# Gated units transposed four blocks at a time, query and key products ahead of value products in the last opening blocks, one activation-table load fewer, and retention's scale issued later

## The chip, the cores and the metric

One NeuronCore of a Trainium2 chip runs the whole program. The metric is the device time of one execution in microseconds (us). The profile calls the engines PE (TensorE), ACT (ScalarE), DVE (VectorE), POOL (GpSimd) and SP (SyncE, which issues the loads); PEld is TensorE's weight load.

## What is computed

A trunk of two layers over 256 tokens of width 1024, in float32. Each layer has a mixer and a gated feed-forward network, both behind an RMS norm and a modulation by a conditioning vector `c`:

```python
for layer in range(2):
    shift_m, scale_m, gate_m, shift_f, scale_f, gate_f = ada_mod(c, ada_w[layer], ada_b[layer])
    h = modulate(rms_norm(x, norm_gains[layer, 0]), shift_m, scale_m)
    y = attn_hybrid_mixer(h, ...) if layer == 0 else retention_mixer(h, ...)
    x = x + gate_m * y
    h = modulate(rms_norm(x, norm_gains[layer, 1]), shift_f, scale_f)
    gt, up = split(h @ w_gate_up[layer], 2)          # 2 x 2816 columns
    x = x + gate_f * ((silu(gt) * up) @ w_down[layer])
out = rms_norm(x, final_norm)
```

The attention mixer has 8 stick-breaking heads (queries, keys and values qs, ks, vs) and 8 rotary softmax heads (qm, km, vm). The retention mixer has 4 heads; each head's output o is normalised over its 512 columns, `(o - mu) * rsqrt(var + 1e-5)`, multiplied by a gain and by `silu(g)`, and goes into the output projection.

## The kernel before

**Tiles and products.** The tokens are two halves of 128, t = 0 and t = 1. A weight unit is 256 rows by 512 columns, two row blocks of 128 wide as one raw tile of 128x1024. To keep float32 precision on TensorE, every operand is split in two fp32r parts: ScalarE copies `wh` out of the raw tile (L221), VectorE takes `wl = raw - wh` (L222), each 512 columns at a time. A row block's product is three matmuls into one accumulator: wh with hh (L440), wl with hh (L441) and wh with hl (L444), where hh and hl are the two parts of the activations. These three lines are most of TensorE's time.

**Stages, with their times in the profiled execution.** Opening, 0 to 68 us: the row blocks kb = 0 to 7 of qs, ks and vs (g = 0, 1, 2), each block's products following as soon as its modulated activations and its split weights are there. Attention, to 161 us: the stick-breaking scores (`sb_task`: L590, L598, then Abs, Exp and Ln on ScalarE at L602 to L604, the maximum on VectorE at L605), the projections qm, km, vm, the softmax part (`moba_part`, transposes at L661) and the output projection. The first feed-forward network, to 355 us, with 11 groups of gated units and then the down projection. Retention, to 536 us: for each of 4 heads the projections rqk, rg, rv and a task for each half (`ret_task`), then the output projection to 560 us. The second feed-forward network, to 751 us.

**Small work between products.** A generator (a task) holds the work that follows a group: transposes, scores, splits. `yield 4` puts a task off by four ticks; each weight unit of each half makes two ticks, one after its first products and one after its L444s, and a task whose count has run out issues its next piece there. `GY`, `R0` to `R2`, `QP` and `SY` are such counts. TensorE's order is therefore the order in which the program is written and ticks. The orders of ScalarE, VectorE, GpSimd and SyncE are made by a list scheduler when the program is built; only what `pin` or `keep_in_program_order` encloses keeps its place.

**The places of the change.** `products(kb, g)` issues the products of block kb for one of qs, ks and vs, both halves. `to_T` (L506, L507) transposes finished queries and keys to the form that the scores want: four transposes, and a copy on ScalarE (L507); for qs and ks a copy out of the accumulator (L515) goes ahead of them. `log_table` issues a load of ScalarE's activation table (L235) with the set that has exp and ln. `gu_post` takes an accumulator of gated units (256 gate columns, 256 up columns): Silu on ScalarE (L802), multiply on VectorE (L803), and `GY` ticks later a run of two transposes (L813) and a split into the activations of the down projection. `ret_task` ends with the normalisation: VectorE takes the moments, GpSimd works out the reciprocal root in steps of one column (`rsqrt`, L207 to L216), ScalarE multiplies by it (L758), and `R2` ticks later TensorE transposes the result.

The weight and ada loads go out on SyncE's one queue: L424 for weight units, L335 for blocks of `ada_w`. VectorE multiplies those `ada_w` blocks by c (L357, 128x1024 each), in between the other work.

Of the kernel before, what the change touches and what calls it, by code (L numbers as in the profile page):

```python
# [14 lines left out]
AF = mybir.ActivationFunctionType  # L15
# [4 lines left out]
P = 128  # L20
# [3 lines left out]
KD = D // P  # L24
# [10 lines left out]
MY, MV = (8, 6), 2  # L35
SY, SV = (7, 7), 4
GY = 4
R0, R1, R2 = 6, 4, 14
QR, QP = 6, 3
GW = 12  # L40
PRIO = 600
# [11 lines left out]
def trunk_kernel(  # L53
# [6 lines left out]
    nc = tc.nc  # L60
# [172 lines left out]
    def log_table():  # L233
        tc.keep_in_program_order(
            nc.scalar.preload_act_table_set("natural_log_exp_and_others"))  # L235
# [331 lines left out]

    def sb_task(t):
        if t == 0:
            log_table()  # L570
        if t == 0:
            st[t]["o"] = tuple(hp.tile([P, KD, P], F32R, tag="oq" + n, name=nm("o" + n))
                               for n in "hl")
        else:
            o = ap.tile([P, 2, KD, P], F32R, tag="B1l", name="o1")
            st[t]["o"] = o[:, 0], o[:, 1]
# [142 lines left out]
    def ret_task(h, t):  # L719
# [35 lines left out]
        v1 = sp.tile([P, 1], F32, tag="v", name=nm("v"))  # L755
        nc.gpsimd.tensor_scalar(v1, mv[:, 1:2], 1e-5, None, op0=ALU.add)
        r = rsqrt(v1)
        nc.scalar.activation(o, o, AF.Copy, scale=r)  # L758
        yield R2
        yield ("ps", 1, 1)  # L760
# [32 lines left out]
        return Blocks(f"{t}h", n), Blocks(f"{t}l", n)  # L793

    def gu_post(l, g):
        key = f"act{l}"

        def f(t, ps):
            if g == 0:
                st[t][key] = act_tiles(t, 22)  # L800
            s = w2(t)
            nc.scalar.activation(s[:, :256], ps[:, :256], AF.Silu)  # L802
            nc.vector.tensor_mul(s[:, :256], s[:, :256], ps[:, 256:])  # L803
            release(1)
            spawn(task(t, s))

        def task(t, s):
            hi, lo = st[t][key]
            yield GY
            yield ("ps", 1, 1)  # L810
            p = pt()
            for j in range(2):
                nc.tensor.transpose(p[:, j * P:(j + 1) * P], s[:, j * P:(j + 1) * P], ident)  # L813
            split(hi[:, 2 * g:2 * g + 2, :].rearrange("p k q -> p (k q)"),
                  lo[:, 2 * g:2 * g + 2, :].rearrange("p k q -> p (k q)"), p[:, :256])
            release(1)
            flags.add((t, key, 2 * g))
            flags.add((t, key, 2 * g + 1))

        return f  # L820

# [253 lines left out]
    def more(upto):  # L1075
        while ready[0] < min(upto, n):
# [6 lines left out]
                ada_load(*e)  # L1083
            ready[0] += 1

    def products(kb, g, ts=(0, 1)):
        kp, j = divmod(kb, 2)
        for t in ts:
            units[g * NP + kp][1](t, *ws[kp, g], js=(j,))

    strict[0] = True
    log_table()
# [124 lines left out]
```

## Time and profile before

| | |
|---|---|
| time, median of 3 runs | 761.07 us (760.92 to 762.19) |
| profiled execution | 761.21 us |
| its span on the chip | 759.4 us |
| TensorE busy | 732.6 us, 96% of the span |
| VectorE busy | 559.7 us, 74% |
| ScalarE busy | 403.2 us, 53% |
| GpSimd busy | 56.4 us, 7% |

A row of the timeline or a group gives its engine, line, operation and the program's names with the buffer numbers left out; `[1.25 <-ACT w L515]` says that the engine stood idle for 1.25 us before the row and that the idle time ended with ScalarE's write of `w` at line 515. Matmuls overlap their neighbours: the distance between two starts is what one costs, not the duration printed. The profiled execution lasts 1.8 us longer than its span, and it is 0.14 us above the median of the runs.

### The profile page before, as it was taken

The numbers are of one execution on the slowest core, as the hardware profiler recorded it, in microseconds if no ns is written. First come the engines' busy times: TensorE is split into PE (matmuls) and PEld (weight loads), VectorE is DVE, ScalarE is ACT, GpSimd is POOL, SyncE is SP. The second block draws the span as 40 slices with busy tenths as digits, with TensorE's granted clock in tenths as the row PEclk, the third lists the DMA queues.
The fourth block names the chain that finished last, engine by engine and source line by source line (L and its number), as shares of the span: only waits on it lengthen the run. The fifth ranks groups of instructions, "written<-read, shape, count | busy, mean of one in ns | idle before, by whom it ended". The sixth has DMA issues, their size and how long they took to land.

```text
span 759.4 us, 10601 instructions
## 1 busy us (share of the span) xinstructions
PE 732.6 (96%) x3598; PEld 581.2 (77%) x3598; DVE 559.7 (74%) x963; ACT 403.2 (53%) x836; POOL 56.4 (7%) x137
## 2 busy tenths in 40 slices
PE   8998997999999999999999999999999999999995
PEld 4776775667888878877788877777877888888884
DVE  3668999689898879857857777676588767665553
ACT  5339745665555545546545454454575555555541
POOL 1001000120000010001011111203020000000000
PEclk9999999999999999999999999999999999999999
DMA  9997889568999979946564737577747777655501
GB/s 297 346 360 253 288 291 331 184 185 271 335 295 342 330 246 326 341 168 194 191 199 146 241 120 224 185 236 240 234 146 224 224 228 213 192 178 181 171 1 55
DMA packets 116998, 174.91 MB, mean 230 GB/s; under 512 B 7640, under 2 KB 73376, under 8 KB 116944
## 3 DMA queue, kind: packets, MB, share of 16 engines
q1 hardware_dynamic: 115568, 171.86, 69.6%
q10 hardware_dynamic: 816, 1.60, 0.6%
q0 software_dynamic: 560, 0.77, 0.3%
q8 instruction: 28, 0.46, 0.3%
q14 instruction: 26, 0.21, 0.1%
HBM read 173.16 MB, written 1.05 MB: 229 GB/s over the span
## 4 chain that ended last, share of the span: by engine, by line
PE 65%; DVE 6%; ACT 2%; issue 2%; POOL 2%; DMA 1%; DVEq 0%; SPq 0%; ACTq 0%; POOLq 0%
PE acc L440 20%; PE acc L444 20%; PE acc L441 20%; DVE wl L222 2%; PE pt L813 1%; ACT wh L221 1%; ACT w L287 1%; DMA raw<-in_ffn_w_gate_up_dram 1%; DVE w L528 0%; PE pt L729 0%; PE pt L746 0%; POOL ra L211 0%; PE pt L506 0%; DVE w L256 0%; ACT w L227 0%
## 5 line engine op out<-in xcount | busy, mean ns | idle before, releaser
L222 DVE TENSOR_TENSOR wl<-raw,wh 128x512 fp32r<-128x512 f32 x456 | 298.0, 688 | 133.6 <-ACT wh L221 131.3
L221 ACT ACTIVATE wh<-raw 128x512 fp32r<-128x512 f32 x456 | 266.2, 623 | 210.0 <-PE acc L444 110.1
L440 PE MATMUL acc<-wh,hh 128*128 128x512 f32 x640 | 258.1, 403 | 3.3 <-ACT hh L963 2.2
L441 PE MATMUL acc<-wl,hh 128*128 128x512 f32 x640 | 250.5, 391 | 0.2 <-DVE wl L222 0.2
L444 PE MATMUL acc<-wh,hl 128*128 128x512 f32 x640 | 204.9, 395 | 1.2 <-DVE hl L291 1.2
L440 PEld LDWEIGHTS acc<-wh,hh 128*128 128x128 f32 x640 | 120.5, 188 | 32.4 <-ACT hh L963 3.8
L444 PEld LDWEIGHTS acc<-wh,hl 128*128 128x128 f32 x640 | 119.1, 188 | 28.2 <-DVE hl L291 2.7
L441 PEld LDWEIGHTS acc<-wl,hh 128*128 128x128 f32 x640 | 120.7, 189 | 24.4 <-DVE wl L222 1.3
L440 PE MATMUL acc<-wh,act 128*128 128x512 f32 x240 | 94.4, 393 | 0.0
L441 PE MATMUL acc<-wl,act 128*128 128x512 f32 x240 | 93.7, 390 | 0.2 <-DVE wl L222 0.2
L444 PE MATMUL acc<-wh,act 128*128 128x512 f32 x240 | 74.2, 390 | 0.0
L357 DVE SCALAR_TENSOR_TENSOR aacc<-raw,sc,aacc 128x1024 f32<-128x1024 f32 x48 | 61.4, 1279 | 0.0
L440 PEld LDWEIGHTS acc<-wh,act 128*128 128x128 f32 x240 | 45.1, 188 | 10.3 <-issue 0.8
L441 PEld LDWEIGHTS acc<-wl,act 128*128 128x128 f32 x240 | 45.1, 188 | 10.0 <-DVE wl L222 0.8
L444 PEld LDWEIGHTS acc<-wh,act 128*128 128x128 f32 x240 | 44.9, 188 | 9.4
L357 DVE SCALAR_TENSOR_TENSOR gate<-raw,sc,gate 128x1024 f32<-128x1024 f32 x32 | 40.9, 1279 | 0.1
L802 ACT ACTIVATE w<-acc 128x256 f32<-128x256 f32 x44 | 16.9, 384 | 28.1 <-PE acc L444 28.1
L803 DVE TENSOR_TENSOR w<-w,acc 128x256 f32<-128x256 f32 x44 | 18.4, 417 | 10.3 <-ACT w L802 10.2
L354 POOL MEMSET aacc<- 128x1024 f32 x6 | 5.6, 966 | 226.8 <-PE pt L387 178.6
L227 ACT ACTIVATE w<-x 128x512 f32<-128x512 f32 x20 | 12.5, 625 | 16.4 <-DVE x L309 15.7
L230 POOL TENSOR_SCALAR ss<-ss 128x1 f32<-128x1 f32 x8 | 2.3, 288 | 250.3 <-ACT w L227 250.3
L758 ACT ACTIVATE w<-w,ry 128x512 f32<-128x512 f32 x8 | 5.8, 724 | 27.3 <-POOL ry L216 27.3
(168 smaller groups left out, 622.0 us busy)
## 6 DMA issues: line engine op xcount, KB each, us to landing
raw<-in_ffn_w_gate_up_dram SPq DMA_DIRECT2D x176, 256.0 KB, 4.3
raw<-in_ada_w_dram SPq DMA_DIRECT2D x80, 512.0 KB, 5.5
raw<-in_ffn_w_down_dram SPq DMA_DIRECT2D x44, 512.0 KB, 5.1
raw<-in_ret_w_in_dram SPq DMA_DIRECT2D x32, 512.0 KB, 3.8
early<-in_ada_w_dram SPq DMA_DIRECT2D x16, 512.0 KB, 7.4
raw<-in_ret_w_in_dram SPq DMA_DIRECT2D x32, 256.0 KB, 3.9
raw<-in_ret_w_o_dram SPq DMA_DIRECT2D x16, 512.0 KB, 5.1
raw<-in_att_w_qkv_dram SPq DMA_DIRECT2D x24, 256.0 KB, 7.2
```

What stands on the lines that cost most here:

```text
L221: pin(nc.scalar.activation(hi, src, AF.Copy))
L222: pin(nc.vector.tensor_tensor(lo, src, hi, op=ALU.subtract))
L227: pin(nc.scalar.activation(w2(t), xt[t][:, half * 512:(half + 1) * 512], AF.Square, scale=1.0 / 32.0, accum_out=ss))
L287: nc.scalar.activation(hs[1][:, c], ps[1][:, c], AF.Identity, scale=gm[:, 4 + j:5 + j], bias=sm[:, 4 + j:5 + j])
L357: tc.keep_in_program_order(nc.vector.scalar_tensor_tensor(a, r, sc[:, kk:kk + 1], a, op0=ALU.mult, op1=ALU.add))
L440: nc.tensor.matmul(ps, hi[:, kb, :], a, start=first, stop=False)
L441: nc.tensor.matmul(ps, hi[:, kb, :], b, start=False, stop=False)
L444: nc.tensor.matmul(ps, lo[:, kb, :], wh[:, j * 512:(j + 1) * 512], start=False, stop=last)
L758: nc.scalar.activation(o, o, AF.Copy, scale=r)
L802: nc.scalar.activation(s[:, :256], ps[:, :256], AF.Silu)
L803: nc.vector.tensor_mul(s[:, :256], s[:, :256], ps[:, 256:])
L813: nc.tensor.transpose(p[:, j * P:(j + 1) * P], s[:, j * P:(j + 1) * P], ident)
```

## The change

It has four parts. In the last two opening blocks (kb = 6 and 7) the value products are held back, and both blocks' are issued after block 7's queries and keys. The call of `log_table` in `sb_task` goes away; the one at the start of the program and those in `resid_post` stay. Two neighbouring gated units of a half share one 512-column tile, and one task transposes and splits all four of its blocks (the last unit, g = 10, is alone and keeps two). In `ret_task` a wait of 8 ticks stands ahead of the scale and `R2` is 6 ticks in place of 14.

```diff
-R0, R1, R2 = 6, 4, 14
+R0, R1, R2 = 6, 4, 6
...
     def sb_task(t):
-        if t == 0:
-            log_table()
...
         r = rsqrt(v1)
+        yield 8
         nc.scalar.activation(o, o, AF.Copy, scale=r)
         yield R2
...
     def gu_post(l, g):
+
         key = f"act{l}"
+        c = slice(g % 2 * 256, g % 2 * 256 + 256)
 
         def f(t, ps):
             if g == 0:
                 st[t][key] = act_tiles(t, 22)
-            s = w2(t)
-            nc.scalar.activation(s[:, :256], ps[:, :256], AF.Silu)
-            nc.vector.tensor_mul(s[:, :256], s[:, :256], ps[:, 256:])
+            if g % 2 == 0:
+                st[t]["gu"] = w2(t)
+            s = st[t]["gu"][:, c]
+            nc.scalar.activation(s, ps[:, :256], AF.Silu)
+            nc.vector.tensor_mul(s, s, ps[:, 256:])
             release(1)
-            spawn(task(t, s))
-
-        def task(t, s):
+            if g % 2 or g == 10:
+                spawn(task(t, st[t]["gu"], 2 * (g - g % 2), 2 + g % 2 * 2))
+
+        def task(t, s, b0, n):
             hi, lo = st[t][key]
             yield GY
             yield ("ps", 1, 1)
             p = pt()
-            for j in range(2):
+            for j in range(n):
                 nc.tensor.transpose(p[:, j * P:(j + 1) * P], s[:, j * P:(j + 1) * P], ident)
...
+    held = []
+
     def products(kb, g, ts=(0, 1)):
-        kp, j = divmod(kb, 2)
-        for t in ts:
-            units[g * NP + kp][1](t, *ws[kp, g], js=(j,))
+        if g == 2 and kb >= KD - 2:
+            held.append(kb)
+            if kb + 1 < KD:
+                return
+        for kb in held if g == 2 and held else (kb,):
+            kp, j = divmod(kb, 2)
+            for t in ts:
+                units[g * NP + kp][1](t, *ws[kp, g], js=(j,))
```

**TensorE at the end of the opening.** `acc_242` and `acc_288` are the query accumulators of the two halves, `acc_246` and `acc_313` those of the keys, `acc_250` and `acc_317` those of the values. Before, block 6's value products stand ahead of block 7's first query products (wh_627):

```order
L441 MATMUL acc_313<-wl_632,hh_239 128x512
L444 MATMUL acc_313<-wh_631,hl_240 128x512
L440 MATMUL acc_250<-wh_635,hh_166 128x512
L441 MATMUL acc_250<-wl_636,hh_166 128x512
L444 MATMUL acc_250<-wh_635,hl_167 128x512
L440 MATMUL acc_317<-wh_635,hh_239 128x512
L441 MATMUL acc_317<-wl_636,hh_239 128x512
L444 MATMUL acc_317<-wh_635,hl_240 128x512
L440 MATMUL acc_242<-wh_627,hh_166 128x512
L441 MATMUL acc_242<-wl_628,hh_166 128x512
L444 MATMUL acc_242<-wh_627,hl_167 128x512
L440 MATMUL acc_288<-wh_627,hh_239 128x512
```

In the changed kernel block 7's queries and keys come first, and then the two value accumulators take block 6 and block 7, one behind the other. The twelve rows ahead of and with the first score (L588, before L590); `pt_765` and `pt_774` are the transposes of the keys of the two halves:

```order
L506 MATMUL pt_765<-mats,w_0_145_742 128x128 x4
L444 MATMUL acc_250<-wh_635,hl_167 128x512
L440 MATMUL acc_317<-wh_635,hh_239 128x512
L441 MATMUL acc_317<-wl_636,hh_239 128x512
L506 MATMUL pt_774<-mats,w_1_147_753 128x128 x4
L444 MATMUL acc_317<-wh_635,hl_240 128x512
L440 MATMUL acc_250<-wh_635,hh_166 128x512
L441 MATMUL acc_250<-wl_636,hh_166 128x512
L444 MATMUL acc_250<-wh_635,hl_167 128x512
L440 MATMUL acc_317<-wh_635,hh_239 128x512
L441 MATMUL acc_317<-wl_636,hh_239 128x512
L588 MATMUL pt_789<-att_sb 128x128
```

The six matmuls of block 6's values have moved behind block 7's keys, and the second half's key transposes (`pt_774`), which stood directly ahead of the first score, now have six matmuls between them and it.

**ScalarE at retention's scale in a task of t = 1, first head.** `wh` are weight splits, and the row with `ry` is the scale by the reciprocal root. Before:

```order
L507 ACTIVATE qk_818_3984<-pt_832_4040 128x4x128
L221 ACTIVATE wh_850_4102<-raw_822_3999 128x512
L221 ACTIVATE wh_853_4122<-raw_833_4046 128x512
L758 ACTIVATE w2_1_840_4071<-w2_1_840_4071,ry_848_4089 128x512
L221 ACTIVATE wh_853_4122<-raw_833_4046 128x512
L221 ACTIVATE wh_859_4150<-raw_849_4100 128x512 x2
L706 ACTIVATE sg_855_4135<-acc_825_4007 128x512
```

After, the same stretch:

```order
L507 ACTIVATE qk_798_3943<-pt_812_3999 128x4x128
L221 ACTIVATE wh_830_4060<-raw_802_3958 128x512
L221 ACTIVATE wh_833_4080<-raw_813_4005 128x512 x2
L757 ACTIVATE w2_1_820_4030<-w2_1_820_4030,ry_828_4048 128x512
L221 ACTIVATE wh_839_4109<-raw_829_4058 128x512 x2
L704 ACTIVATE sg_835_4094<-acc_805_3966 128x512
```

One weight split of 128x512 (the second half of one weight tile, wh_853 before and wh_833 after) has come from behind the scale to ahead of it; all else in the stretch keeps its place.

**SyncE's queue at 90 us.** L424 loads attention weights, L335 loads blocks of `ada_w`. Before:

```order
L424 DMA raw_1018<-in_att_w_qkv_dram 128x2x512
L335 DMA raw_973<-in_ada_w_dram 128x1024
L424 DMA raw_1053<-in_att_w_qkv_dram 128x2x512
L335 DMA raw_1027<-in_ada_w_dram 128x1024
L335 DMA raw_1030<-in_ada_w_dram 128x1024
L424 DMA raw_1094<-in_att_w_qkv_dram 128x2x512
L335 DMA raw_1062<-in_ada_w_dram 128x1024
```

After:

```order
L424 DMA raw_1017<-in_att_w_qkv_dram 128x2x512
L335 DMA raw_972<-in_ada_w_dram 128x1024
L335 DMA raw_1026<-in_ada_w_dram 128x1024
L335 DMA raw_1029<-in_ada_w_dram 128x1024
L424 DMA raw_1052<-in_att_w_qkv_dram 128x2x512
L424 DMA raw_1093<-in_att_w_qkv_dram 128x2x512
L335 DMA raw_1061<-in_ada_w_dram 128x1024
```

One weight load (raw_1053 before, raw_1052 after) now stands behind two more `ada_w` loads.

## Rows read from the trace of the kernel before

**Rows 1.** The page of the profiled execution: the span, busy time with its share of the span and the number of instructions by engine, and the two groups that split the weights (line, engine, operation, out<-in, count, busy us and mean ns of one, idle before).

```profile
span 759.4 us, 10601 instructions
...
PE 732.6 (96%) x3598; PEld 581.2 (77%) x3598; DVE 559.7 (74%) x963; ACT 403.2 (53%) x836; POOL 56.4 (7%) x137
...
L222 DVE TENSOR_TENSOR wl<-raw,wh 128x512 fp32r<-128x512 f32 x456 | 298.0, 688 | 133.6 <-ACT wh L221 131.3
L221 ACT ACTIVATE wh<-raw 128x512 fp32r<-128x512 f32 x456 | 266.2, 623 | 210.0 <-PE acc L444 110.1
```

**Rows 2.** The timeline of TensorE around the last two opening blocks: start and duration in us, engine, line, operation, out<-in, shape, count, and in brackets the idle time before and what ended it.

```profile
56.88 0.39 PE L440 MATMUL acc<-wh,hh 128*128 128x512 f32 x1
...
58.24 0.39 PE L440 MATMUL acc<-wh,hh 128*128 128x512 f32 x1
...
63.23 0.40 PE L441 MATMUL acc<-wl,hh 128*128 128x512 f32 x1
64.88 0.66 PE L506 MATMUL pt<-mats,w 128*128 128x128 f32 x4 [1.25 <-ACT w L515]
66.41 1.68 PE L590 MATMUL pt<-att_sb 64*128 64x128 f32 x16 [0.87 <-ACT att_sb L507]
...
69.28 0.63 PE L440 MATMUL acc<-wh,hh 128*128 128x512 f32 x1
```

**Rows 3.** Four equal stretches around the first attention scores, two of them: busy us and instructions of each engine, then the granted clock of TensorE, the share of DMA and GB/s.

```profile
63.50:66.90 3.40, 1.28 (x13) 0.92 (x14) 3.40 (x5) 3.38 (x8) 0.00 (x0) 1.00 0.91 322
66.90:70.30 3.40, 3.40 (x18) 2.52 (x17) 2.81 (x4) 3.39 (x6) 0.00 (x0) 0.50 0.83 299
```

**Rows 4.** The timeline of ScalarE from block 7's first weight split to the first attention exponentials.

```profile
56.78 1.66 ACT L221 ACTIVATE wh<-raw 128x512 fp32r<-128x512 f32 x3
...
64.23 0.60 ACT L515 ACTIVATE w<-acc 128x512 f32<-128x512 f32 x1
...
66.86 1.28 ACT L235 ACT_TABLE_LOAD   x1
68.16 0.60 ACT L507 ACTIVATE att_sb<-pt 128x512 f32<-128x512 f32 x1
68.72 1.08 ACT L602 ACTIVATE w<-pt 128x512 f32<-128x512 f32 x2
```

**Rows 5.** The timeline of VectorE at block 7's first low weights and at the first attention maximum, and the busy times of the stretch from 72 to 130 us (columns as in rows 3).

```profile
57.42 0.69 DVE L222 TENSOR_TENSOR wl<-raw,wh 128x512 fp32r<-128x512 f32 x1 [0.23 <-ACT wh L221]
...
71.39 1.29 DVE L605 SCALAR_TENSOR_TENSOR sps<-pt,w 128x512 f32<-128x512 f32 x2 [1.65 <-ACT w L604]
...
72.00:130.00 58.00, 54.38 (x299) 39.98 (x298) 55.67 (x78) 35.45 (x78) 0.00 (x0) 1.00 0.91 306
```

**Rows 6.** The timeline of TensorE at its two longest waits of the attention stage.

```profile
124.99 0.63 PE L661 MATMUL pt<-mats,w 128*128 128x128 f32 x4 [1.72 <-DVE w L650]
126.97 0.63 PE L661 MATMUL pt<-mats,w 128*128 128x128 f32 x4 [1.35 <-DVE w L650]
```

**Rows 7.** The queue of SyncE at 90 us, the group of its attention-weight loads (KB each, us from issue to landing), and VectorE's low weights of one of them.

```profile
89.95 0.38 SPq L424 DMA_DIRECT2D raw<-in_att_w_qkv_dram  x1
91.15 2.13 SPq L335 DMA_DIRECT2D raw<-in_ada_w_dram  x2
...
raw<-in_att_w_qkv_dram SPq DMA_DIRECT2D x12, 512.0 KB, 5.3
...
104.48 1.29 DVE L222 TENSOR_TENSOR wl<-raw,wh 128x512 fp32r<-128x512 f32 x2
```

**Rows 8.** The timeline of TensorE at two runs of transposes between products: the two products just before a run of two transposes (L813) and the product after the next, and the same around a run of four (L506).

```profile
195.17 0.62 PE L444 MATMUL acc<-wh,hl 128*128 128x512 f32 x2
...
196.09 0.40 PE L441 MATMUL acc<-wl,hh 128*128 128x512 f32 x1
...
379.99 0.62 PE L444 MATMUL acc<-wh,hl 128*128 128x512 f32 x2
...
381.12 0.39 PE L441 MATMUL acc<-wl,hh 128*128 128x512 f32 x1
```

**Rows 9.** The timelines around retention's scale in the second half's first task (ScalarE, VectorE), the three waits of TensorE that follow such tasks, and single GpSimd steps of the reciprocal root.

```profile
412.26 0.72 ACT L758 ACTIVATE w<-w,ry 128x512 f32<-128x512 f32 x1 [2.74 <-POOL ry L216]
...
409.56 0.69 DVE L222 TENSOR_TENSOR wl<-raw,wh 128x512 fp32r<-128x512 f32 x1 [0.40 <-ACT wh L221]
413.54 0.69 DVE L222 TENSOR_TENSOR wl<-raw,wh 128x512 fp32r<-128x512 f32 x1 [3.29 <-ACT wh L221]
...
418.35 0.68 DVE L533 TENSOR_TENSOR w<-w,w 128x512 f32<-128x512 f32 x1
...
419.18 0.41 PE L506 MATMUL pt<-mats,w 128*128 128x128 f32 x2 [0.38 <-DVE w L533]
...
458.60 0.41 PE L506 MATMUL pt<-mats,w 128*128 128x128 f32 x2 [0.66 <-DVE w L533]
...
498.51 0.41 PE L506 MATMUL pt<-mats,w 128*128 128x128 f32 x2 [0.60 <-DVE w L533]
...
409.78 0.61 POOL L214 TENSOR_SCALAR rb<-rb,ra 128x1 f32<-128x1 f32 x1
...
411.59 0.27 POOL L214 TENSOR_SCALAR rb<-rb,ra 128x1 f32<-128x1 f32 x1
...
513.26 1.11 POOL L213 TENSOR_SCALAR rb<-ra 128x1 f32<-128x1 f32 x1
```

More of the change, by code (lines that the diff above doesn't have):

```diff
@@ L811, in task @@
             p = pt()
-            for j in range(2):
+            for j in range(n):
                 nc.tensor.transpose(p[:, j * P:(j + 1) * P], s[:, j * P:(j + 1) * P], ident)
-            split(hi[:, 2 * g:2 * g + 2, :].rearrange("p k q -> p (k q)"),
-                  lo[:, 2 * g:2 * g + 2, :].rearrange("p k q -> p (k q)"), p[:, :256])
+            split(hi[:, b0:b0 + n, :].rearrange("p k q -> p (k q)"),
+                  lo[:, b0:b0 + n, :].rearrange("p k q -> p (k q)"), p[:, :n * P])
             release(1)
-            flags.add((t, key, 2 * g))
-            flags.add((t, key, 2 * g + 1))
+            for j in range(n):
+                flags.add((t, key, b0 + j))
         return f
```

## The prediction, made blind

> **What bounds the kernel now.** I read the page first. TensorE is busy for 96% of the span, VectorE for 74%, ScalarE for 53% [rows 1], so what the change does elsewhere counts only where TensorE waits for it, or where it takes work off TensorE. The page gives an average, so I then went through TensorE's timeline place by place and looked for rows with idle time in brackets and for distances between starts that are longer than the usual one. That usual distance follows from the six value products of block 6, whose first starts at 56.88 us and whose successor starts at 58.24 [rows 2]: 1.36 / 6 = 0.227 us a product. Three places touch the change. At the end of the opening TensorE waits 1.25 us ahead of the last key transposes and 0.87 us ahead of the first scores [rows 2]. Right after these waits its granted clock is 0.50, the 1.2 GHz level, for the stretch 66.90 to 70.30, while it is 1.00 in the stretch before, in which TensorE worked 1.28 of 3.40 us [rows 3]. In retention it waits behind three of the tasks of the second half, 0.38, 0.66 and 0.60 us [rows 9]. All of it together is under 1% of the time.
>
> **Opening: products held back.** The six value products leave the place ahead of block 7's queries, so TensorE wants these at 56.88 in place of 58.24. Their high weights aren't there: ScalarE starts the first of three splits at 56.78, and one takes 0.62 [rows 1, 4], so 57.40, a wait of some 0.55 with the signal. The low weights start at 57.42 on VectorE and take 0.69 [rows 5], so 58.1: another 0.45. This wait of about 1.0 us is new. The wait of 1.25 ahead of the second half's key transposes followed the copy L515, which runs from 64.23 to 64.83 behind two weight splits [rows 2, 4]. In the changed kernel the copy has only its key products ahead of it, and TensorE meets the transposes earlier; I estimate 0.4 us that remain. But then six value products stand between these transposes and the scores, which cover ScalarE's copies of the keys, so the 0.87 goes. The sum ahead of the scores is 1.25 + 0.87 = 2.12 less, 1.0 + 0.4 = 1.4 more, and a little that the waits cost beside their idle time (the start at 64.88 is 1.65 after the one before, where 0.227 is usual, so 1.42 for 1.25 of idle [rows 2]). I expect the first score at 65.4 to 65.6 instead of 66.41: a lead of 0.9.
>
> **The clock.** In the stretch at 0.50 TensorE was busy for all of its 3.40 us [rows 3]; at full clock the same would take half, so 1.7 us are at stake. It fell after the two waits that stood in one stretch of 3.4 us. In the changed kernel the waits are shorter and 6 us apart, and I expect full clock there. TensorE's lead is then 0.9 + 1.7 = 2.6 us by 70.3.
>
> **What of that lead lasts.** VectorE takes the attention maximum at 71.39 behind ScalarE's Abs, Exp and Ln [rows 5]. ScalarE's chain gains 1.28 from the table load that goes (66.86; the next instruction starts at 68.16, 0.02 after its end), and about 0.4 from the earlier copies [rows 4]: 1.7 us. From 72 to 130 us VectorE is busy for 55.67 of 58.00 us [rows 5], so TensorE can't run ahead of it for long: the smaller lead counts. I take **-1.7 us** for the first two parts and the table load, with the bounds 0 (VectorE has no room at all and earlier loads are not there earlier) and -2.6.
>
> The Trainium skill, "ScalarE: Activation LUTs", section "What ACT_TABLE_LOAD costs", puts a switch at 1283 ns and a drain of 1380 ns besides. The trace agrees with the first figure (1.28) and shows no drain here. By the skill's page ScalarE would win 2.66 us, and the sum could come out 1.4 lower.
>
> **Gated units in pairs.** Eleven units by two halves by two layers are 44 runs of two transposes; they become 20 runs of four and 4 of two. The start of the product pair ahead of a run of two to the second product behind it is 196.09 - 195.17 = 0.92 us, and 381.12 - 379.99 = 1.13 around a run of four [rows 8]. Without transposes three products take 0.68. So a run of two costs 0.24, a run of four 0.45, and each pairing saves 0.48 - 0.45 = 0.03: 20 x 0.03 = 0.6, and with the reading error of the starts **-0.5 us**. ScalarE and VectorE save more (one split of 512 columns in place of two of 256), but off the path. A pair's first half is ready one unit later than before; the last unit is alone, so the down projection's last blocks come as early as they did. I cost that at nothing: the down projection takes the blocks in order, and the first of them are tens of us old. Bounds 0 and -0.6.
>
> **Retention's scale.** ScalarE stood for 2.74 us ahead of the scale at 412.26, because GpSimd's reciprocal root was not ready [rows 9]. Nothing but one weight split changes sides, and only in the four tasks of the second half. That split can run in the 2.74 us. VectorE's low weights, which came at 413.54 after 3.29 us of idle [rows 9], are then some 0.6 after the split before them, near 410.1, VectorE's other work follows on, and it comes to L533, for which TensorE waited at 419.18, over 1 us sooner than 418.35. So the three waits, 0.38 + 0.66 + 0.60 = 1.64, may go. Against it: GpSimd's steps last until a long VectorE operation beside them ends. The step at 409.78 took 0.61 beside the low weights of 409.56, the same step at 411.59 took 0.27; the one at 513.26 took 1.11 [rows 9]. With more VectorE work moved into this window the root is later by 0.3 (0.61 - 0.27) to 0.9 a task, and the scale and the splits behind it with it. I take the first wait gone and some 0.3 of each of the other two kept or passed on: 0.4 + 0.35 + 0.35 = **-1.1 us**, bounds 0 and -2.1 (the 1.64 and the time beside the idle, in the ratio 1.42 to 1.25 of the opening, with a reserve of 0.2).
>
> On this the Trainium skill has a rule, "SBUF — State Buffer", section "Who interferes with whom": a VectorE instruction with two inputs in SBUF and a GpSimd instruction that reads SBUF want the same port, and the one that comes second is blocked until the other ends. It speaks against this change; the stretched steps agree with it. By it alone the root could lose all that the split gains, which is rival D below.
>
> **SyncE.** One weight load moves behind two ada loads. It was issued at 89.95 and now goes about 3.4 us later (91.15 + 2.13 = 93.28), lands 5.3 later, at 98.6 [rows 7]; I take the 0 to 1.7 of lead off that. VectorE first needs its low part at 104.48 [rows 7], 0.7 less for ScalarE's split: 5 us of slack. Cost nothing; with the cover gone it would cost up to 3.4.
>
> **Sum.** -1.7 - 0.5 - 1.1 = -3.3 on the profiled 761.2, so 757.9; the median is 0.14 below the profiled execution: **757.8 us**. A measurement of this kernel can tell about 0.2%, 1.5 us, from no change, so faster means below 759.55.
>
> **Rivals.**
> A, the forecast: 757.8, its own range 756.0 (both larger bounds half met) to 759.0; chance 0.48.
> B, the opening's lead is eaten by VectorE and the loads before 130 us: 757.8 + 1.7 = 759.5. For it speaks VectorE's 96% in that stretch; against it, that VectorE's own chain starts earlier. 0.20.
> C, the lead is kept, but the clock falls at another place. Nearest are the waits of 1.72 and 1.35 at 124.99 and 126.97 [rows 6], 2 us apart as those of the opening were, and longer if TensorE comes earlier; the clock stayed at 1.00 [rows 5]. One more stretch at 0.50 costs 1.7: 759.5. 0.10.
> D, the scale's move does nothing: one split moves, GpSimd's steps stretch by as much: 757.8 + 1.1 = 758.9. 0.14.
> E, slower: the weight load behind the ada loads lands after VectorE wants it, TensorE waits, and the opening's lead is lost in the same wait. It decides from a landing later than about 103.8, 5 us after my estimate. 761.1 + 3.4 - 0.5 - 1.1 = 762.9. 0.08.
>
> The range 755.4 to 760.2 takes in B, C and D whole and A down to the larger bounds of the opening (-0.9) and retention (-1.0) and half a microsecond of the drain; outside remain E and a tenth for what no row shows. B and C lie on the bound of faster, so their 0.30 is halved; of A and D, 0.04 may end above it. Faster 0.73, same 0.19, slower 0.08.
>
> **What would show it.** The clock full from 66 to 71 us; the first score near 65.5 and the first maximum near 69.7; TensorE's waits of 1.0 at block 7's queries and 0.4 at the keys; the last gated unit's products 0.25 sooner against its stage's start in each layer; retention's three waits under 0.2 together with scales that come later by 0.3 to 0.9. Wrong I would be if the first maximum is earlier but the softmax part at 125 us is not, if a clock row of 0.50 stands anywhere new, or if rows of TensorE show new waits for weight loads between 98 and 110 us.

## The result, and the profile after

The changed kernel takes 755.82 us (median of 4 runs, 754.61 to 756.81) against 761.1 for the kernel before: a ratio of 0.9933, with a 95% interval of 0.9917 to 0.9949. That is 5.3 us or 0.7% faster; the forecast was 757.8 with a range of 755.4 to 760.2. A second set of runs of the same changed kernel, described below, gave 756.38 us and a ratio of 0.9942 (0.9922 to 0.9961).

The page of the changed kernel's profiled execution (756.01 us) has the same picture as [rows 1]. The weight splits are as many and as long as they were, and TensorE is busy for 1.5 us less:

```profile
span 754.2 us, 10567 instructions
...
PE 731.1 (97%) x3598; PEld 582.1 (77%) x3598; DVE 557.6 (74%) x943; ACT 399.8 (53%) x815; POOL 58.7 (8%) x137
...
L222 DVE TENSOR_TENSOR wl<-raw,wh 128x512 fp32r<-128x512 f32 x456 | 297.5, 687 | 131.1 <-ACT wh L221 127.7
L221 ACT ACTIVATE wh<-raw 128x512 fp32r<-128x512 f32 x456 | 265.2, 623 | 207.6 <-PE acc L444 128.6
```

The end of the opening answers to [rows 2]. TensorE now waits for block 7's weights at 57.34 and 58.07, for the key copy only 0.22 us at 63.58, and the first scores start at 65.56:

```profile
57.34 0.49 PE L440 MATMUL acc<-wh,hh 128*128 128x512 f32 x1 [0.39 <-ACT wh L221]
58.07 0.50 PE L441 MATMUL acc<-wl,hh 128*128 128x512 f32 x1 [0.23 <-DVE wl L222]
...
63.58 0.66 PE L506 MATMUL pt<-mats,w 128*128 128x128 f32 x4 [0.22 <-ACT w L515]
...
65.56 1.16 PE L588 MATMUL pt<-att_sb 64*128 64x128 f32 x16
```

The two stretches of [rows 3], in the changed kernel: TensorE works 3.32 of 3.40 us in the first, and in the second its granted clock (the figure after the engines' busy times) is 1.00, the 2.4 GHz level, where it was 0.50:

```profile
63.50:66.90 3.40, 3.32 (x28) 2.54 (x29) 3.40 (x4) 3.40 (x8) 0.00 (x0) 1.00 0.88 306
66.90:70.30 3.40, 3.40 (x16) 2.80 (x15) 3.04 (x5) 3.34 (x8) 0.00 (x0) 1.00 0.86 313
```

ScalarE's and VectorE's side, to be held against [rows 4, 5]. There is no table load between the copy L875 and the first Abs (L600), and the first attention maximum stands at 69.81 where it stood at 71.39:

```profile
66.44 0.63 ACT L875 ACTIVATE att_v<-acc 128x512 f32<-128x512 f32 x1
67.13 1.08 ACT L600 ACTIVATE w<-pt 128x512 f32<-128x512 f32 x2
...
69.81 1.29 DVE L603 SCALAR_TENSOR_TENSOR sps<-pt,w 128x512 f32<-128x512 f32 x2 [0.32 <-ACT w L602]
```

### The profile page after: what moved, and what is told of

It is laid out like the page before. It is cut to its first block, busy times and chain, and to the rows that moved or that the text cites. A ratio compares the mean times of both kernels' runs of the same rounds, so it can differ in the third digit from the quotient of the medians.

```text
span 754.2 us, 10567 instructions
## 1 busy us (share of the span) xinstructions
PE 731.1 (97%) x3598; PEld 582.1 (77%) x3598; DVE 557.6 (74%) x943; ACT 399.8 (53%) x815; POOL 58.7 (8%) x137
## 4 chain that ended last, share of the span: by engine, by line
PE 67%; DVE 5%; POOL 2%; issue 2%; ACT 2%; DVEq 0%; ACTq 0%; POOLq 0%
PE acc L444 21%; PE acc L440 21%; PE acc L441 21%; DVE wl L222 2%; PE pt L817 1%; DVE w L256 1%; DVE gate L357 0%; PE pt L727 0%; PE pt L744 0%; PE pt L506 0%; PE pt L278 0%; DVE w L528 0%; ACT wh L221 0%; ACT w L287 0%; POOL ra L211 0%
## 5 line engine op out<-in xcount | busy, mean ns | idle before, releaser
L357 DVE SCALAR_TENSOR_TENSOR aacc<-raw,sc,aacc 128x1024 f32<-128x1024 f32 x48 | 61.3, 1278 | 0.0
L357 DVE SCALAR_TENSOR_TENSOR gate<-raw,sc,gate 128x1024 f32<-128x1024 f32 x32 | 40.9, 1278 | 0.1
```

What stands on the lines that cost most here:

```text
L357: tc.keep_in_program_order(nc.vector.scalar_tensor_tensor(a, r, sc[:, kk:kk + 1], a, op0=ALU.mult, op1=ALU.add))
```

## The experiments

In the first four, one part of the change is made to the kernel before. One theory takes the forecast's terms as they stand; the other puts the gain of attention down to waits much later in that stage, which in the changed kernel's trace were gone too.

**Value products held back, alone.** Edit: only the `held` part of the diff.

> The kernel before with only the value products of the last two opening blocks held back; the table load ahead of the first attention exponentials stays. Theory 1 (the prediction's: waits and clock of the opening): the waits of 1.25 and 0.87 us ahead of the first scores shrink to under 0.5 together, the granted clock stays at 1.00 from 66 to 71 us, TensorE is about 2.3 us ahead at 82 us, but ScalarE's 1.28 us stays in the chain, so only 0.5 to 1.2 us of that last to the end of attention: 759.9 to 760.6 us. Theory 2 (the gain of the changed kernel in attention comes from places later than the opening: the softmax waits of 0.8 and 0.45 us at 142 us go because the output-projection loads on SyncE stand in another order and because VectorE's small steps no longer meet GpSimd's clearing of two tiles at 138 us): whatever the lead at 82 us is, the gain at 170 us is over 2 us only if both waits at 142 us are gone in this trace too; if they stay, under 1.5 us.

Measured: 763.79 us against 760.73, ratio 1.004 (1.0026 to 1.0054). This part alone makes the kernel slower by 3 us. The opening did what was expected: the granted clock is 1.00 from 60.0 to 73.7 us, and with the start of the first product taken as zero TensorE is 1.9 us ahead at 82 us. But at 162 us it is 2.5 us behind. In between, ScalarE waits three times over 3 us for weight loads. TensorE is still 1.8 us ahead at 110 us, after all three. It loses 4.2 us from 112 to 118 us, at its own two waits for VectorE (the last two rows); besides, its granted clock is 0.50 for 3.4 us from 115.6 on:

```profile
96.19 0.63 ACT L221 ACTIVATE wh<-raw 128x512 fp32r<-128x512 f32 x1 [3.13 <-DMA raw<-in_att_w_qkv_dram]
...
102.92 1.15 ACT L221 ACTIVATE wh<-raw 128x512 fp32r<-128x512 f32 x2 [3.11 <-DMA raw<-in_att_w_qkv_dram]
107.55 0.63 ACT L221 ACTIVATE wh<-raw 128x512 fp32r<-128x512 f32 x1 [3.48 <-DMA raw<-in_att_w_o_dram]
...
112.44 0.50 PE L441 MATMUL acc<-wl,hh 128*128 128x512 f32 x1 [0.69 <-DVE wl L222]
...
116.12 1.08 PE L506 MATMUL pt<-mats,w 128*128 128x128 f32 x4 [2.11 <-DVE w L533]
```

The order of SyncE's loads differs, and with it ScalarE's and VectorE's. It isn't the sum of ScalarE's waits for loads: from 68 to 165 us it is 21.0 us here and 21.3 in the kernel before. Below are 70 loads from the opening to the first feed-forward stage (Q attention weights, O output projection, g gate and up, a an `ada_w` block, a dot another load):

```
before               QQaa..aQQQaaQaQQaaQaaQQaaQaQaaQaOagaOaaOagOaaaOOggaOaOggggaggggggggggg
held alone           QQaa..aQQQaaQaQQaaQaaQQaQaaQaaQaOgaaOaaOaOaaOaOgggaOaOggaggggggggggggg
held, no table load  QQaa..aQQQaaQaQQaaQaaQaQaQaaaQQaOagaOaaOagOaaaOOggaOOggaggaggggggggggg
changed kernel       QQaa..aQQQaaQaQQaaQaaQaQaQaaaQQaOagaOaaOagOaaaOOggaOOggaggaggggggggggg
```

Neither theory had this: the gain at 82 us was there, and it was not only lost but turned round.

**The table load taken away, alone.** Edit: only `log_table()` in `sb_task`.

> The kernel before without the table load of the first attention task, all else in its place and the loads on SyncE in the same order. Theory 1: the first scores don't move, the granted clock still falls to 0.50 for about 3.4 us after them, the first attention maximum comes up to 1.28 us sooner, TensorE is under 0.5 us ahead at 82 us; 760.3 to 761.0 us. Theory 2: the waits at 142 us stay, since neither the order of loads nor the distance between VectorE and GpSimd there changes by more than 1.28 us; 760.0 to 761.1 us. By the drain that the notes add to a load the maximum would come 2.6 us sooner, and the time could reach 759.

Measured: 761.4 us against 760.73, ratio 1.0002 (0.9992 to 1.0012): nothing. ScalarE's time goes into a wait of 1.52 us ahead of Abs. The profile names no releaser for it (`issue`), but Abs needs the scores, whose last matmul starts only at 68.06; they come late and at 0.54 of the clock (the last row, 66.90 to 70.30):

```profile
66.61 0.63 ACT L507 ACTIVATE att_sb<-pt 128x512 f32<-128x512 f32 x1
68.76 1.09 ACT L600 ACTIVATE w<-pt 128x512 f32<-128x512 f32 x2 [1.52 <-issue]
...
66.90:70.30 3.40, 3.40 (x18) 2.57 (x17) 2.72 (x4) 1.88 (x5) 0.00 (x0) 0.54 0.78 295
```

So the load was hidden behind the slow scores. Neither 2.66 us nor a part of them shows. In the kernel before, this load also brought in a set that was already in place: no other table load stands between the one at 4.32 us and it. So it was no switch to another set.

**Gated units paired, alone.** Edit: only `gu_post`.

> The kernel before with only the gated units paired. Theory 1: TensorE gains 0.03 us a pairing, 0.2 to 0.3 us in each of the two feed-forward stages and nothing elsewhere: 760.5 us (760.3 to 760.8). Rival: the pairs' later transposes or the loads that change places on SyncE cost as much as the shorter runs save: 761.0 or more.

Measured: 760.64 us, ratio 0.9994 (0.9982 to 1.0006). The interval covers the forecast's 0.5 us and zero. The traces tell more, because the feed-forward stages scatter little: over eleven traces (all but held products alone and the two forced collisions below) the first one (from that stage's early products to the first of retention) takes 182.61 us on average with pairs and 182.76 without, the stretch from the end of retention's heads to the end 222.84 and 223.12. That is 0.14 + 0.28 = 0.4 us. No rival cost shows.

**Retention's scale later, alone.** Edit: `yield 8` and `R2 = 6`.

> The kernel before with only retention's scale issued 8 ticks later. Theory 1: the three waits after the second half's tasks (0.38, 0.66, 0.60 us idle) get shorter by about 0.3 each and the time in retention falls by 1.1 to 1.4 us: 759.8 us (759.5 to 760.2). Rival: the gain of retention in the changed kernel came from an earlier start of its loads or an order that the other parts brought: then 760.6 to 761.1 us here.

Measured: 759.98 us, ratio 0.9988 (0.9977 to 0.9998), 0.9 us faster. Of the same eleven traces, the four with the changed scale take 170.38 us on average for the retention heads (169.98 to 170.80), the six without it 171.70 (171.18 to 172.59): 1.3 us. The trace of this run alone has 170.80, 0.9 less than these six.

**Both parts of the opening.** Edit: `held` and no `log_table()` in `sb_task`.

> The two parts of the opening together: value products held back and no table load; gated units and retention as before. Its loads stand on SyncE in the order of the changed kernel up to the end of attention. Theory 1 (the parts add up: the held products cost 3 us alone, the load nothing): about 763.8 us. Theory 2 (what decides is the order that the list scheduler gives the loads between 85 and 130 us, which the table load's 1.28 us in the scheduler's plan turned in the run with held products alone): TensorE is over 2 us ahead at 82 us and over 2.5 us ahead at 170 us, no wait over 1 us between 110 and 118 us; 756.8 to 758.2 us.

Measured: 757.89 us against 760.97, ratio 0.9964 (0.995 to 0.9978). One part alone cost 3 us, the other did nothing; together they gain 2.7. The parts don't add up. But that doesn't yet say whether the table load or the order did it:

**The table load put back in another place.** The kernel with both opening parts, and:

```diff
+            if (kb, g) == (5, 2):
+                log_table()
             if kb >= KD - 2:
                 if (kb, g) in ((KD - 2, 2), (KD - 1, 0), (KD - 1, 1)):
```

> As the kernel with both opening parts, but with the table load put back at another place: after block 5's value products, where ScalarE stands idle for 2.6 us anyway. Six loads as before the change, and every other instruction of ScalarE, VectorE and SyncE in the order of the kernel with both opening parts. Theory 2 (order of the loads): the same time as that kernel within 0.8 us, 756.8 to 758.2. Rival (the load itself, its 1.28 us and what it does to the functions after it, is what the changed kernel saves): 1.3 to 2.7 us more than that kernel.

Measured: 758.5 us against 760.97, ratio 0.9972 (0.9962 to 0.9981). That is 0.6 us more than without the load: within the 0.8 that theory 2 allows, though above its 758.2, and the intervals of the two ratios overlap. The rival's 1.3 us is unlikely but not quite ruled out by them. The load runs where ScalarE waits anyway:

```profile
53.43 1.28 ACT L235 ACT_TABLE_LOAD   x1
56.04 0.57 ACT L961 ACTIVATE hh<-w 128x128 fp32r<-128x128 f32 x2 [1.32 <-DVE w L959]
```

There are as many loads as before the change, and all else stands in the order of the kernel with both opening parts. So it isn't the number of table loads that decides. With the load at its old place, what follows stands in another order, and the kernel is 5.9 us slower (763.79 against 757.89). The load's own 1.28 us can be only a part of that: at 82 us, where the loads on SyncE still stand in the same order, TensorE's lead is 1.9 us with it and 2.3 without. No run has the load at its old place and the good order, so the order as the cause of the rest is argued from this difference. Whether SyncE's order, ScalarE's or VectorE's does more harm isn't separated, since all three turn together.

**The softmax waits at 142 us.** In the execution before, TensorE waited twice behind VectorE's softmax rows, and these behind an odd row: two negations of 128x2 maxima that took 1.66 us together, with the clearing of two tiles by GpSimd beside them (GpSimd, VectorE and TensorE in turn). The second wait is put down to ScalarE's split, which ended last; VectorE's L650 for it ended at 142.94, 0.15 us ahead of the start, the same distance as at the first:

```profile
138.10 1.85 POOL L354 MEMSET aacc<- 128x1024 f32 x2 [78.21 <-PE pt L387]
...
138.31 1.66 DVE L642 TENSOR_SCALAR mx<-mx 128x2 f32<-128x2 f32 x2
138.44 1.54 DVE L650 TENSOR_TENSOR w<-w,rc 128x512 f32<-128x512 f32 x1
...
142.18 0.63 PE L661 MATMUL pt<-mats,w 128*128 128x128 f32 x4 [0.64 <-DVE w L650]
143.09 0.41 PE L661 MATMUL pt<-mats,w 128*128 128x128 f32 x2 [0.28 <-ACT wh L221]
```

In the changed kernel the same negations were over before the clearing began:

```profile
135.50 0.21 DVE L640 TENSOR_SCALAR mx<-mx 128x2 f32<-128x2 f32 x2
...
136.87 1.85 POOL L354 MEMSET aacc<- 128x1024 f32 x2 [77.08 <-PE pt L387]
```

The form of the negation was changed in the kernel before, with a tile of zeros:

```diff
-            nc.vector.tensor_scalar(mx[:, :per], mx[:, :per], -1.0, None, op0=ALU.mult)
+            nc.vector.tensor_tensor(mx[:, :per], zero4[:, :per], mx[:, :per], op=ALU.subtract)
```

> The kernel before with one operation in another form: the softmax's negation of the maxima (128 by 4 or 2) is a subtraction from a tile of zeros instead of a multiplication by -1; order and loads as before. Theory: in the profiled execution of before, GpSimd's clearing of two tiles (138.10 us, 1.85) held VectorE's multiplication from 138.31 to its end, 1.5 us, and TensorE waited 0.8 and 0.45 us at 142 us for it; the subtraction isn't held, so these waits are gone and runs of over 761.5 us get rare: median 759.9 to 760.4. Rival (VectorE was held by something else, or TensorE has slack there): the operation after the clearing is held as before, or the median stays within 0.2 us of that of before.

Measured: 759.42 us against 760.97, ratio 0.9984 (0.9968 to 0.9999). The runs reach from 757.1 to 762.0, so those over 761.5 didn't go, and in this trace the negation had ended before the clearing. The time alone doesn't prove the cause. So the collision was forced, with either form:

```diff
+            if t == 1:
+                nc.vector.tensor_copy(scr[0][:, 0:1], zp[par][:, 0:1])
+                for _ in range(1):
+                    nc.gpsimd.memset(scr[0], 0.0)
             mx = sp.tile([P, 4], F32, tag="mx", name=nm("mx"), bufs=4)
...
```

> The kernel before with the collision forced: in the second half's softmax a copy of one column ahead of each of the four maxima releases a clearing by GpSimd of a spare tile of 128 by 1024 (0.96 us by the rows of before), so that the negation of the maximum falls into it. The negation is the multiplication of before. Theory (the clearing holds that form): three or four of the four negations end only with the clearing, 0.3 to 1.5 us in place of 0.16, and what follows on VectorE is held too; TensorE waits longer in the softmax part of 130 to 145 us. Rival (VectorE is held by something else, such as a result of ScalarE): the negations take 0.16 us as ever.

> The same forced clearings, but the negation is the subtraction from a tile of zeros. Instructions stand in the same order on every engine. Theory: all four negations take under 0.3 us inside the clearings, and the copies of one column are the only ones that may be held. Rival (any small VectorE operation that meets a clearing is held): the same 0.3 to 1.5 us as with the multiplication.

Measured: 764.06 us with the multiplication, 763.19 with the subtraction, one run each. The added rows also put SyncE's loads in another order than in the kernel before, the same in both, so these times are not to be held against that kernel's; the rows are what counts. First and last negation of the former, with the clearings beside them; each ends when the clearing does (135.86 + 0.96 and 136.38 + 0.46, 142.51 + 0.97 and 142.85 + 0.66):

```profile
135.86 0.96 POOL L643 MEMSET scr<- 128x1024 f32 x1 [75.32 <-ACT wh L221]
...
142.51 0.97 POOL L354 MEMSET aacc<- 128x1024 f32 x1
...
136.38 0.46 DVE L646 TENSOR_SCALAR mx<-mx 128x2 f32<-128x2 f32 x1
...
142.85 0.66 DVE L646 TENSOR_SCALAR mx<-mx 128x2 f32<-128x2 f32 x1
```

The same with the subtraction, inside the clearings, 0.16 and 0.15 us:

```profile
137.03 0.95 POOL L645 MEMSET scr<- 128x1024 f32 x1 [77.30 <-ACT wh L223]
...
143.44 0.97 POOL L356 MEMSET aacc<- 128x1024 f32 x1
...
137.55 0.16 DVE L648 TENSOR_TENSOR mx<-zero,mx 128x2 f32<-128x2 f32 x1
...
143.78 0.15 DVE L648 TENSOR_TENSOR mx<-zero,mx 128x2 f32<-128x2 f32 x1
```

All four multiplications were held (0.46, 0.40, 0.40, 0.66), no subtraction was. The cause of the hold is shown. The Trainium skill, "SBUF — State Buffer", section "Who interferes with whom", names `tensor_scalar` among the operations that can take the pair of ports that VectorE and GpSimd share, while a `tensor_tensor` with two inputs in SBUF contends with GpSimd's reads and not with an instruction that only writes. The trace agrees with both: a clearing only writes, and it held the multiplications and not the subtractions.

**The changed kernel with the subtraction.**

> The changed kernel with the negation as a subtraction, which a clearing doesn't hold. In the changed kernel's profiled execution the last negation ended 1.2 us ahead of the clearing, so theory 1 (it has that margin in most executions): no gain, 755.0 to 756.3 us. Theory 2 (its other executions collide as those of before do): up to 1 us less, 754.5 to 755.3, and the slowest runs below 756.5.

Measured: 755.97 us, the changed kernel's time. Theory 1 holds: in both traces of the changed kernel itself the multiplications end ahead of the clearing anyway. In the execution before, the collision made waits of 0.64 and 0.28 us of idle time (0.8 and 0.45 by the starts), but it doesn't settle when a stage ends. Of three other traces that had it, one (before) was among the two latest of its order at the end of attention, but two (both opening parts, and the control below) were among the three earliest of theirs.

**Retention's scale four ticks later, as a control.** The changed kernel with `yield 4` and `R2 = 10`.

> The changed kernel with retention's scale only 4 ticks later (and the transposes 10 ticks after it) in place of 8 and 6. ScalarE's order around the eight scales is then that of the kernel before: no weight split changes sides. Theory (the gain of retention is that one split in the tasks of the second half): the waits after the second half's first three tasks are as before, 0.4 to 0.7 us idle each, and retention takes 0.9 to 1.4 us longer than in the changed kernel. Rival (the gain comes from the later scale or its transposes as such): waits of 0.2 to 0.4 and the changed kernel's time in retention.

Measured: 757.36 us in one run. Retention's heads take 171.55 us, against 170.48 in the changed kernel: the gain of 1.1 us is gone with the one split. The first of the three waits is back:

```profile
415.91 0.52 PE L506 MATMUL pt<-mats,w 128*128 128x128 f32 x3 [0.37 <-DVE w L533]
```

The other two were no different from those of the changed kernel (0.55 and 0.54 us beyond the usual distance, against 0.54 and 0.53); the rest was lost elsewhere in the stage. So the expectation held for the sum and for one wait of three.

**The changed kernel again.**

> The changed kernel once more, with more executions, since its first four stand against forecasts that differ by about 1 us. Theory 1 (the parts add up as they were measured alone, -2.4 to -3.0 for the opening, -0.5 for the pairs, -0.9 for the scale): 756.4 to 757.2 us median beside 760.3 to 761.1 for the kernel before. Theory 2 (together they gain more than apart): 755.2 to 756.2. In the profiled execution the distance from GpSimd's first clearing to the last negation of the maxima decides again whether there is a wait of 0.8 us in the softmax part: a negation that starts after the clearing is held to the end of both clearings, one that ends before it is not.

Measured: 756.38 us against 760.65, at the edge between the two theories. The last negation ended at 136.40, 0.35 us ahead of the clearing.

## Why the prediction was right

**The opening (waits).** Right in place and size: the new wait before block 7's products was put at 1.0 us and is 0.39 + 0.23 of idle time, or 0.55 + 0.50 by the distances between starts; the remaining wait for the key copy was put at 0.4 and is 0.22 idle, 0.38 by the starts; the first score was expected at 65.4 to 65.6 and came at 65.56.

**The clock.** Right at that place: 1.00 from 60.0 to 73.7 us. The table load doesn't lower it: with held products and the load it stays at 1.00, without the load and with the waits it falls to 0.54. But the waits don't lower it in every execution. With the old opening it fell to 0.50 at 66 to 68 us in five of seven traces. In the other two (pairs alone, and the forced collision with the multiplication) the same waits of 1.25 and 0.87 us are there, yet the clock stayed at 1.00, and TensorE was 1.5 us earlier at 71 us than in the profiled execution before. With held products it stayed at 1.00 at that place in all seven traces. So the 1.7 us were there to be won in most executions, not in each.

Rival C happened as well, in the changed kernel's own trace. The two waits that the rival named are 1.57 and 1.27 us here (they end at 123.33 and 125.23), and from 124.70, within the second, the granted clock is 0.50 for 3.4 us (columns as in [rows 3]):

```profile
121.30:124.70 3.40, 1.09 (x7) 0.46 (x5) 3.40 (x7) 1.91 (x12) 0.00 (x0) 1.00 1.00 362
124.70:128.10 3.40, 2.87 (x9) 2.51 (x10) 3.40 (x6) 3.40 (x7) 0.00 (x0) 0.50 1.03 371
```

TensorE's lead over the execution before fell from 1.7 to 0.4 us in this stretch, and 0.8 of it was back at 131 us. The execution before had worked 0.99 of 3.40 us at the same place and kept 1.00. Nine of all fourteen traces, with either opening, have such a fall between 124 and 130 us. So the forecast read one execution's clock as the kernel's, and C's chance of 0.10 was too low. Its price of 1.7 us is hardly to be seen at the end of the stage where the fall was a single one (next paragraph).

**What of the lead lasts, -1.7.** Right in size, partly wrong in its course. VectorE's first maximum came 1.58 us sooner; after it VectorE's weight splits were 1.3 to 2.8 us ahead up to 105 us, and VectorE as a whole 1.66 from 109 to 124 us. Over the traces, the time from the first product to a fixed product early in the first feed-forward stage (172.97 us before) is 158.91 us on average with the old opening (five traces, 157.45 to 160.16) and 157.10 with the new order (six, 156.41 to 158.81): 1.8 us, by their scatter known to about 1.6 either way, and the two groups overlap. The two profiled executions themselves differ by 3.2 there, because that of before is one of the late ones of its kind. That scatter between executions of nearly one order of instructions, up to 2.7 us in this stage, was not in the forecast's range as a cause; the forecast took one execution for the rule. It goes with the low clock up to that product: with the new order the traces without a fall have 156.49 and 156.50, those with 3.4 us at 0.50 have 156.41 to 157.73, the one with 6.8 us has 158.81; with the old order 3.4 us go with 157.45 to 159.91, 6.8 us with 159.49 and 160.16. No run sets the clock apart from the rest, so it isn't shown as the cause. With the dearer table load that the forecast also prices, the sum would by its own rule (the smaller lead counts, and TensorE's ends at 2.6) have come out 0.9 us lower, not 1.4.

**SyncE, cost nothing.** Here a step failed. The forecast asked when VectorE needs the weights of the load that moves behind two `ada_w` loads, and found 5 us of slack. It forgot its own question for a wait: what is queued behind it. The load itself came when the forecast said: it was put at 98.6, and ScalarE's split of that weight starts at 98.80, after a wait of 4.87 us. But the two copies of the attention weights (L612) stand behind that split, and TensorE waits for the second of them at the product with the values (in turn SyncE, ScalarE, TensorE):

```profile
87.43 4.52 SPq L335 DMA_DIRECT2D raw<-in_ada_w_dram  x3
92.05 2.99 SPq L424 DMA_DIRECT2D raw<-in_att_w_qkv_dram  x2
...
98.80 0.63 ACT L221 ACTIVATE wh<-raw 128x512 fp32r<-128x512 f32 x1 [4.87 <-DMA raw<-in_att_w_qkv_dram]
99.34 0.58 ACT L612 ACTIVATE prob<-pt 128x512 f32<-128x512 f32 x1
100.85 0.59 ACT L612 ACTIVATE prob<-pt 128x512 f32<-128x512 f32 x1
...
101.49 0.77 PE L551 MATMUL pt<-prob,att_v 128*64 128x128 f32 x10 [0.62 <-ACT prob L612]
```

TensorE had been 2.0 us ahead from 90 us on and was 1.0 ahead at 104. So rival E's mechanism is there, but it took 1.0 us, not the whole lead, and TensorE got half of it back (1.5 us ahead at 115 us) where the execution before waited for VectorE. With held products alone the time was rival E's, 763.79 us against 762.9, but by the waits at 112 and 116 us shown above and not at this load. Its chance of 0.08 was low for a change whose load order depends on the scheduler's plan.

**Pairs, -0.5.** Right: 0.4 by the stages. A run of four in the changed kernel, from the pair of products ahead of it to the second product behind it, takes 192.55 - 191.42 = 1.13 us, as the run of four in [rows 8]:

```profile
191.42 0.62 PE L444 MATMUL acc<-wh,hl 128*128 128x512 f32 x2
191.88 0.60 PE L817 MATMUL pt<-mats,w 128*128 128x128 f32 x4
...
192.55 0.40 PE L441 MATMUL acc<-wl,hh 128*128 128x512 f32 x1
```

**The scale, -1.1.** Right in the sum, 1.3 by the stages and 0.9 by the runs (0.2 to 1.75). In the changed kernel's first such task, ScalarE's scale, VectorE, GpSimd, and TensorE's three waits:

```profile
410.15 0.72 ACT L757 ACTIVATE w<-w,ry 128x512 f32<-128x512 f32 x1 [3.65 <-POOL ry L216]
...
406.00 1.29 DVE L222 TENSOR_TENSOR wl<-raw,wh 128x512 fp32r<-128x512 f32 x2 [0.40 <-ACT wh L221]
407.21 1.28 DVE L357 SCALAR_TENSOR_TENSOR gate<-raw,sc,gate 128x1024 f32<-128x1024 f32 x1
...
406.22 1.13 POOL L214 TENSOR_SCALAR rb<-rb,ra 128x1 f32<-128x1 f32 x1
407.45 1.20 POOL L216 TENSOR_SCALAR ry<-ry,rb 128x1 f32<-128x1 f32 x1
...
415.26 0.41 PE L506 MATMUL pt<-mats,w 128*128 128x128 f32 x2
...
454.73 0.52 PE L506 MATMUL pt<-mats,w 128*128 128x128 f32 x3 [0.38 <-DVE w L533]
...
494.34 0.52 PE L506 MATMUL pt<-mats,w 128*128 128x128 f32 x3 [0.38 <-DVE w L533]
```

The first wait is all but gone, the other two keep 0.38 us each, near the 0.3 that the sum took. (The sign that the forecast gave, under 0.2 us for all three together, doesn't fit that sum and wasn't met.) These two waits scatter: in the ten traces with the scale at its old place or 4 ticks later they are 0.36 to 0.66 us, so the 0.66 and 0.60 that the forecast read lie at the top, and less was to be won there. The reciprocal root, from its first step on GpSimd to the scale, lasts 5.24, 4.34, 4.33 and 4.14 us in the four tasks of the second half, where it lasted 3.81, 4.01, 4.01 and 3.85: longer by 1.43, 0.33, 0.32 and 0.29. The forecast had 0.3 to 0.9; in the first task both the split and L357 fell into it, and GpSimd's steps took 1.13 and 1.20 in place of 0.27 and 0.28. That the split runs ahead of the scale was worth more. So rival D was half right: the cost is there, the gain is larger. Part of the gain came where it wasn't looked for, in the wait at the end of the fourth head (518.65 us before), which went; it is gone in all four traces with the new scale, and scatters between nothing and 0.5 us (by the starts) in the others.

**The sum.** By the stages: -1.8 - 0.4 - 1.3 = -3.5, against a forecast of -3.3. By the timed runs it is 4.3 to 5.3; the parts measured alone add up to 2.7 + 0.5 + 0.9 = 4.1. The rest, about 1 us, isn't explained: the interval of the opening's ratio alone reaches from 1.7 to 3.8 us, and the scatter of the attention stage is as large. It stays open.

**The signs of being wrong.** The forecast named three. The softmax part at 125 us did come earlier, by 1.7 us. The other two occurred: a row of 0.50 at a new place, and a new wait of TensorE that a weight load brought between 98 and 110 us. So the time fell into the range although two effects that the forecast had put at nothing or called unlikely were there; in part this is luck, since neither is seen in the time at which the stage ends.

## What to carry to other kernels

Where a list scheduler orders the loads, an edit that is free on its engine can still move every load behind it: read the new order of each queue, ask of each load that moves what stands behind the split that waits for it, and time parts together as well as alone. Waits close together just ahead of a dense stretch can cost twice, once themselves and once in the clock of what follows (here 1.5 us between two executions with the same waits). And one profiled execution isn't the rule: set the same stage of several traces side by side before a difference of one or two microseconds is put down to a cause.

## What the runs showed of the hardware

A clearing of a tile by GpSimd (128x1024, 0.96 us) holds a VectorE `tensor_scalar` on 128x2 in SBUF until it ends. Two clearings in a row held it through both in three traces (1.6 to 1.7 us), while in the third forced collision it was let go as the first ended (0.40 us). All that VectorE has behind it stands too; the same sum as a subtraction of two SBUF tiles is not held (0.16 us). And a table load of 1.28 us, taken away ahead of the operations that use it, was worth nothing on its own, since ScalarE then only waited for scores that were late. TensorE's clock after the same two waits (1.25 and 0.87 us) fell to 0.50 in five executions and stayed at 1.00 in two.
